# Half-width value products of two attentions, chained into one stretch per group

## The chip, the cores and the metric

The program runs on one NeuronCore of one Trainium2 chip. The engines are named as in the profile: PE is TensorE (matmuls), PEld its weight loads, DVE is VectorE, ACT is ScalarE, POOL is GpSimd, and SP issues most of the DMAs. The metric is the device time of one execution in microseconds (us), lower is better. The kernel before has a median of 2237.99 us over 3 runs (2236.0 to 2239.27).

## What is computed

A sequence of 2048 tokens with 1024 features passes two blocks, all in float32. The first is a gated linear attention (GLA) layer. The second projects the normalised tokens into three mixers, joins their outputs and projects them back. The change lies in two of these mixers, and in a scratch tile of the final projection:

```python
# sliding-window attention: 6 heads in 2 key/value groups of 3, a window of 128
scores = jnp.einsum('bnqkgd,bnskd->bnkgqs', qb, kk) * (A_DH ** -0.5)   # 128 queries x 256 keys
probs = softmax(scores + alibi, with a sink)
out = jnp.einsum('bnkgqs,bnskd->bnqkgd', probs, vv)                    # 64 features a head

# stick-breaking attention: 4 heads of 64, every query against all keys before it
z = jnp.einsum('bhqd,bhsd->bhqs', qb, kh) * (S_DH ** -0.5)
log_keep = jnp.where(strict, jax.nn.log_sigmoid(-z), 0.0)
suffix = lax.cumsum(log_keep, reverse=True) - log_keep
a = jnp.where(strict, jnp.exp(jax.nn.log_sigmoid(z) + suffix), 0.0)
out = jnp.einsum('bhqs,bhsd->bhqd', a, vh)                             # the value product
```

## The kernel before

The tokens go through in 8 tiles of 256. After the GLA block the second block runs as four stages, one behind the other: the sliding-window stage (some 960 to 1250 us of the profiled execution), the mLSTM stage (to some 1635 us), the stick-breaking stage (to 2131 us) and the output projection, half of whose tiles already run beside the last stick-breaking tiles.

Within a stage, `pipeline` sets three streams side by side for each tile: `mix` (the attention of tile t), `gate` (of tile t) and `dense` (the projections of tile t + 1, from `dense3_steps`; in the last tile the first projections of the next stage). The streams are only written interleaved. The order in which each engine gets its instructions is chosen afterwards by a scheduler, which follows the dependences, priorities (`high_priority`) and its own estimate of times. So the dense matmuls on tiles named `mm` fill PE between the attention's steps, and an added ordering edge can move instructions of every engine in that stage. Each engine then works strictly through its list. The dense matmuls use a one-pass 32-bit format (F32R); transposes and value products are plain F32, and each of those stands in the trace as two MATMUL instructions, so x2 in a row is one product or one transpose.

A stick-breaking group (`stick_rows`) is 128 queries, two heads (h = 0 and 1) and up to four key blocks of 128. For each head it makes scores into PSUM (tile `z`, two matmuls of the function `qk`), two sigmoids on ACT (`ke`, `be`), a running product along the keys on DVE (`TENSOR_TENSOR_SCAN` on `ke`), a multiplication into `be` (DVE, every fourth on POOL), up to four PE transposes into the PSUM tile `aT`, and a copy to the SBUF tile `aT`: by ACT for h = 0, by DVE for h = 1, which is made last. Then come the value products, two for each key block. A product takes 128 keys to 64 features, so it uses half the columns of the PE array: head 0 writes partitions 0 to 63 of the PSUM tile `po`, head 1 writes 64 to 127. There are 80 groups: 56 of eight products, and 8 each of six, four and two; 544 products in all. Two streams of groups (b = 0 and 1) are interleaved.

A sliding-window block (`swa_rows`) is 128 queries. Its products are likewise half-width, 128 keys to 64 features, but for three heads at once (384 columns). There are two key blocks (sb) and two key/value groups (kv), so four products a block, and two in the first block; 62 in all. Each takes a transposed tile `pT`, which comes out of PSUM by ACT for kv = 0 and by DVE for kv = 1.

`Bank.mm` issues a product. For the first product on a half of the bank it sets the flag that clears it, and puts every later one of that half behind that first in the order (`behind`: order on the engine alone, no wait). Nothing else orders the products: in the stick-breaking code they are written key block by key block, h = 0 first, and the scheduler may put each wherever its own operand is ready. The sliding-window code issues its products with plain matmuls:

```python
for sb in range(2 - nb, 2):
    for kv in range(2):
        mm(po[kv * 64:kv * 64 + 64, :, :], v[n - 1 + sb][:, kv * 64:kv * 64 + 64], pTs[sb, kv],
           start=sb == 2 - nb, stop=sb == 1)
```

In the output projection (`out2_tiles`) ACT squares the PSUM tile `py` into a scratch tile `ysq`, only for its row sums, and DVE writes `y` from the same PSUM tile.

Of the kernel before, what the change touches and what calls it, by code (L numbers as in the profile page):

```python
# [26 lines left out]
def interleave(a, na, b, nb):  # L27
    """run the generators a (na steps) and b (nb steps) side by side"""
    ia = ib = 0
    while a is not None or b is not None:  # L30
        if b is None or (a is not None and ia * nb <= ib * na):
            if next(a, StopIteration) is StopIteration:
                a = None
            ia += 1
        else:
            if next(b, StopIteration) is StopIteration:
                b = None
            ib += 1


class Bank:
    """accumulation groups side by side in one PSUM bank: its first matmul clears the bank"""
# [4 lines left out]
    def mm(self, out, a, b, stop=False, part=0):  # L47
        first = self.first.get(part)
        i = self.k.nc.tensor.matmul(out, a, b, start=first is None, stop=stop, skip_group_check=True).ins  # L49
        if first is None:  # L50
            self.first[part] = i
        else:
            self.k.behind(i, first)


class ConstPool:
    """single tiles by name"""
# [8 lines left out]
class K:  # L66
# [45 lines left out]
    def open(self, ctx, name, bufs=2, side=None):  # L112
        """SBUF of a phase"""
        return ctx.enter_context(self.tc.tile_pool(name=name, bufs=bufs, side=side, reuse_waits="tile"))

    def psum(self, ctx, name, **banks):
        """the PSUM banks of a phase by tag; mm: beside the two lasting ones"""
# [3 lines left out]
    def behind(self, ins, before):  # L121
        """issue order on one engine, no wait"""
# [3 lines left out]
    def table(self, name):  # L126
        """the activation tables that the following Exp, Ln or Sigmoid use"""
# [22 lines left out]
    def weights(self, src, name, stage=None, pool=None, k0=0, k1=None, more=None):  # L150
        """src: DRAM [128, k, n]; returns the hi and lo parts of rows k0 to k1. stage: gives the staging tiles;
        more: DRAM [128, k, m] of further columns"""
# [24 lines left out]
    def pipeline(self, n, load, dense, nd, gate, ng, mix, nm, first, lead=0, nxt=None, pri=0):  # L177
        """beside mix(t) run gate(t, h of t) and dense(t + 1, h of t + 1); load(t) gives h two tiles ahead.
        nd, ng, nm(t): the steps of dense, gate and mix; lead: gate goes first for so many t;
        first: h of tile 0 and its dense, begun or None. nxt: what follows: its load(0), its weights, its dense  # L180
        and the steps of it that go here; returns h, weights and the dense begun"""
# [36 lines left out]
    def ahead(self, steps, n):  # L218
        """the steps, their instructions picked as if they stood n earlier"""
# [7 lines left out]
    def load_hl(self, src):  # L227
        """src: DRAM hi and lo [128, NK, T] each"""
# [9 lines left out]
    def load_h(self, src, pool, n, bufs, tag="hf"):  # L238
        """src: DRAM [128, NK, T] -> hi, lo; by n rows"""
# [5 lines left out]
    def split_h(self, parts, B=None):  # L245
        """parts: (k, float32 [128, n, T]) -> hi, lo of them, plus the columns B if given"""
# [17 lines left out]
    def dense3(self, out, a, ca, b, cb):  # L264
        """out = sum over k of a[:, k, ca].T @ b[:, k, cb], float32 from three passes."""
# [3 lines left out]
    def dense3_steps(self, out, a, ca, b, cb):  # L269
        """the same, with a stop in the middle"""  # L270
# [9 lines left out]
    def rstd(self, out, ss, n):  # L280
        """out = (ss / n + EPS) ** -0.5"""
# [4 lines left out]
    def silu_col(self, src, n, name):  # L286
        """silu of a [128, n] tile by exp and ln."""
# [8 lines left out]
    def matvec(self, pool, w, c, col0):  # L296
        """acc[p, j] = sum over k of c[k * 128 + p] * w[k * 128 + p, col0 + j], j < 512"""
# [11 lines left out]
    def mod_cols(self, pool, stage, w, c, name, at):  # L309
        """columns: G = g * (1 + scale), B = shift, each [128, NK] (feature k * 128 + p). at: (k, what to do there)"""  # L310
# [43 lines left out]
    def transposed(self, xs, tag):  # L354
        """xs: two [128, D] token tiles -> (k, two rows of 128 features in a PSUM bank)"""
# [8 lines left out]
    def make_h(self, pool, banks, G, B, tags=(("hn", 2),) * 4):  # L364
        """banks: of transposed tokens (already scaled by rstd) -> float32 times the columns G, plus B if given,
        by two rows of 128 features"""
# [15 lines left out]
    def x_rstd(self, wk, i, keep):  # L382
        """token-major x, or its squares, and the rstd of its rows"""
# [20 lines left out]
    def x_normed(self, wk, t, G):  # L404
        """feature-major x times rstd and the columns G, by two rows of 128 features"""
# [12 lines left out]
    def gla_consts(self, wk):  # L418
# [7 lines left out]
        # the gate's low-rank part, token-major: hi, hi, lo, each with a column for the bias  # L426
# [76 lines left out]
    def late_mod(self, wk, j):  # L503
        """512 columns of: gate of block 1, shift, scale and gate of block 2"""
# [28 lines left out]
    def gla_dense(self, wk, t, hs, W, st):  # L533
# [6 lines left out]
        # token-major v and r; the low-rank gate  # L540
# [6 lines left out]
        if t % NT == 0:  # L547
            # its rows from partition 0 and 64: hi, from 32: lo, to meet the gate's hi, lo and hi
# [78 lines left out]
        # v of the second head  # L627
# [8 lines left out]
    def gla_gate(self, wk, t, hs, W, st):  # L636
        """silu of r"""
# [11 lines left out]
    def gla_mix(self, wk, t, st, ST):  # L649
# [4 lines left out]
        # scores of both heads and both 128-token chunks  # L654
# [75 lines left out]
    def units(self, key):  # L730
        """loads of the four weight units of a phase"""
# [3 lines left out]
    def halves(self, W):  # L735
        """units of half the rows -> all rows"""
# [66 lines left out]
    def fm(self, out, W, c0, hs):  # L803
        """feature-major block: out [128 columns from c0, T]"""
        self.dense3(out, W, slice(c0, c0 + 128), hs, slice(0, T))

    def stack_k(self, ka, kb, pk, cols):
        """pk [128, T]: two heads on the partition halves; their hi and lo parts, each head stacked on 128"""
# [6 lines left out]
    def stack_q(self, qs, pq):  # L815
        """pq [128, T]: two heads on the partition halves. qs [128, 4, T]: by head, hi on both halves;
        then by head, lo on the half of its k's hi, zero on the other"""
# [8 lines left out]
    def qk(self, out, qs, h, qt, ks):  # L826
        """out = q.T @ k of head h; ks: columns of its stacked k"""
# [81 lines left out]
    def stick_rows(self, wk, n, b, q, i, kst, v, zero, y, st, po, bank):  # L909
        """queries n * 128 .. of heads 2b and 2b + 1 against all keys before them, from the last chunk back"""  # L910
# [5 lines left out]
        while end > 0:  # L916
# [3 lines left out]
            aTs = []  # L920
            for h in range(2):
# [26 lines left out]
                aT = wk.tile([128, 4, 128], F32, name="aT", tag="aT", bufs=3)  # L948
                if h == 0:
                    nc.scalar.activation(aT[:, 0:nb, :], pa[:, 0:nb, :], AF.Copy)  # L950
                else:
                    nc.vector.tensor_copy(aT[:, 0:nb, :], pa[:, 0:nb, :])  # L952
                aTs.append(aT)
            for j in range(nb):
                for h in range(2):
                    c = (2 * b + h) * 64
                    bank.mm(po[h * 64:h * 64 + 64, :], v[:, s0 // 128 + j, c:c + 64], aTs[h][:, j, :],
                            s0 == 0 and j == nb - 1, h)
# [7 lines left out]
    def silu_exp(self, out, src, tmp):  # L966
        """out = src * sigmoid(src), tmp of the same shape"""
# [99 lines left out]
    def swa_rows(self, wk, n, i, qs, kst, v, bias, sink, y, st):  # L1067
# [48 lines left out]
        for sb in range(2 - nb, 2):  # L1116
            for kv in range(2):
                mm(po[kv * 64:kv * 64 + 64, :, :], v[n - 1 + sb][:, kv * 64:kv * 64 + 64], pTs[sb, kv],
                   start=sb == 2 - nb, stop=sb == 1)
# [4 lines left out]
    def mlstm_stats(self, wk, t, g, mp):  # L1124
        """g: gate pre-activations [128, chunk, 8] of tile t -> per-token exponents by chunk and head:
        for the columns, for the state, exp(-m)"""
# [70 lines left out]
    def mlstm_dense(self, t, hs, W):  # L1197
# [8 lines left out]
        def values():  # L1206
            """v, token-major with a column of ones, and the gates"""
# [50 lines left out]
        # q and k of each head  # L1258
# [50 lines left out]
    def mlstm_chunk(self, wk, c, i, st, Cs, hg):  # L1309
# [44 lines left out]
        # h = num / max(|den|, exp(-m)), normed over the head  # L1354
# [30 lines left out]
    def out2_tiles(self, wk, W, hs, t0, t1, bufs, rstd):  # L1385
# [4 lines left out]
        for t in range(t0, t1):  # L1390
            hn = load(t + 1) if t + 1 < NT else None
            for i in range(2):
# [3 lines left out]
                for half in range(2):  # L1396
# [4 lines left out]
                    sq = wk.tile([128, 512], F32, name="ysq", tag="ysq", bufs=1)  # L1401
# [123 lines left out]
```

## Time and profile before

| | before |
|---|---|
| median of 3 runs | 2237.99 us (2236.0 to 2239.27) |
| profiled execution, span from first to last instruction | 2235.3 us |
| PE busy | 2131.8 us, 95% |
| PE weight loads busy | 1902.3 us, 85% |
| DVE busy | 1356.7 us, 61% |
| ACT busy | 902.1 us, 40% |
| POOL busy | 857.7 us, 38% |

The profile is of one execution. Busy PE time is modelled, since matmuls are pipelined: a row's own duration overlaps the next row's, and what a piece of PE work costs is read from the starts of successive rows. In a timeline, the first number is the start of the first instruction of a row, xN the number of merged instructions, and a bracket at the end is idle time of the engine and what ended it. L49 is the matmul line of `Bank.mm`, L276 to L278 are the three dense matmuls, L829 and L830 the scores, L947 the stick-breaking transposes, L1108 and L1118 the transposes and products of the sliding window.

### The profile page before, as it was taken

How to read it: one execution, taken by the hardware profiler on the slowest of the kernel's cores; microseconds unless marked ns; L12 is line 12 of the kernel's file. 1: busy time of each engine (PE TensorE's matmuls, PEld its weight loads, DVE VectorE, ACT ScalarE, POOL GpSimd, SP SyncE). 2: the span in 40 equal slices, each digit the busy share in tenths (PEclk: the TensorE clock that was granted, in tenths of full speed). 3: DMA queues.
4: the chain of work that ended last, by engine and by line, in shares of the span. 5: the costliest groups of instructions: out<-in, count | busy, mean ns of one | idle time of the engine just before them, and what ended most of it. 6: DMA issues, size and time to landing. Idle time of an engine off the chain costs nothing. (4 is left out here: it accounts for less than half of the span.)

```text
span 2235.3 us, 39197 instructions
## 1 busy us (share of the span) xinstructions
PE 2131.8 (95%) x14912; PEld 1902.3 (85%) x14912; DVE 1356.7 (61%) x2517; ACT 902.1 (40%) x2290; POOL 857.7 (38%) x1362
## 2 busy tenths in 40 slices
PE   6999999999999999899999999889799999999998
PEld 6899998899998788797888898888798888777787
DVE  6755756566656466564545455445456688788843
ACT  3534334333333333354545343433445555554411
POOL 3522335322223455553324322232445454573410
PEclk9999999999999999999999999989899999999999
DMA  9522313423322566751214322332441111122252
GB/s 321 178 67 73 126 55 114 123 82 99 91 67 91 195 210 225 241 165 53 90 46 145 98 65 72 84 99 67 121 130 43 44 44 43 44 67 81 67 175 99
DMA packets 122412, 240.00 MB, mean 107 GB/s; under 512 B 13248, under 2 KB 39782, under 8 KB 122224
## 3 DMA queue, kind: packets, MB, share of 16 engines
q1 hardware_dynamic: 108400, 187.17, 27.1%
q0 software_dynamic: 13824, 50.34, 7.1%
q8 instruction: 117, 1.92, 0.4%
q14 instruction: 71, 0.58, 0.1%
HBM read 178.66 MB, written 58.79 MB: 106 GB/s over the span
## 5 line engine op out<-in xcount | busy, mean ns | idle before, releaser
L937 DVE TENSOR_TENSOR_SCAN ke<-ke,zero 128x512 f32<-128x512 f32 (+3 forms) x160 | 186.9, 1182 | 25.9 <-POOL ke L932 14.1
L276 PE MATMUL mm<-hh,u1h 128*128 128x256 f32 x640 | 189.1, 296 | 0.0
L278 PE MATMUL mm<-hh,u1l 128*128 128x256 f32 x640 | 187.9, 294 | 0.0
L277 PE MATMUL mm<-hl,u1h 128*128 128x256 f32 x640 | 186.6, 292 | 0.0
L276 PE MATMUL mm<-u0h,hh 128*128 128x272 f32 (+2 forms) x464 | 155.1, 334 | 5.7 <-POOL hh L260 3.6
L278 PE MATMUL mm<-u0h,hl 128*128 128x272 f32 (+2 forms) x464 | 153.9, 332 | 0.6 <-DVE hl L261 0.4
L277 PE MATMUL mm<-u0l,hh 128*128 128x272 f32 (+2 forms) x464 | 153.6, 331 | 0.0
L276 PE MATMUL mm<-hh,u2h 128*128 128x256 f32 x512 | 147.3, 288 | 0.8 <-DVE gs L564 0.5
L277 PE MATMUL mm<-hl,u2h 128*128 128x256 f32 x512 | 146.4, 286 | 0.0
L278 PE MATMUL mm<-hh,u2l 128*128 128x256 f32 x512 | 145.7, 286 | 0.0
L278 PEld LDWEIGHTS mm<-hh,u1l 128*128 128x128 f32 x640 | 126.0, 197 | 1.3 <-issue 0.9
L276 PEld LDWEIGHTS mm<-hh,u1h 128*128 128x128 f32 x640 | 126.0, 197 | 0.7 <-issue 0.2
L277 PEld LDWEIGHTS mm<-hl,u1h 128*128 128x128 f32 x640 | 125.6, 196 | 0.7 <-issue 0.3
L276 PE MATMUL mm<-u3h,hh 128*128 128x256 f32 (+1 forms) x384 | 124.3, 324 | 0.8 <-DVE vl L546 0.8
L278 PE MATMUL mm<-u3h,hl 128*128 128x256 f32 (+1 forms) x384 | 123.3, 321 | 0.0
L277 PE MATMUL mm<-u3l,hh 128*128 128x256 f32 (+1 forms) x384 | 122.7, 319 | 0.0
L49 PE MATMUL po<-aT,sv 128*64 128x128 f32 x1088 | 108.9, 285 | 6.6 <-DVE aT L952 4.9
L134 ACT ACTIVATE be<-z 128x512 f32<-128x512 f32 (+3 forms) x160 | 86.0, 538 | 68.3 <-PE aT L947 68.0
L276 PE MATMUL mm<-hh,u3h 128*128 128x256 f32 x384 | 110.4, 287 | 0.5 <-POOL u3h L147 0.5
L277 PE MATMUL mm<-hl,u3h 128*128 128x256 f32 x384 | 110.3, 287 | 0.0
L278 PE MATMUL mm<-hh,u3l 128*128 128x256 f32 x384 | 109.3, 285 | 0.2 <-DVE mprev L1189 0.2
L134 ACT ACTIVATE ke<-z 128x512 f32<-128x512 f32 (+3 forms) x160 | 86.1, 541 | 54.8 <-PE z L830 33.1
(419 smaller groups left out, 6983.9 us busy)
## 6 DMA issues: line engine op xcount, KB each, us to landing
hh<-h2Th POOLq DMA_DIRECT2D x48, 512.0 KB, 6.0
hl<-h2Tl POOLq DMA_DIRECT2D x48, 512.0 KB, 5.3
mvw<-in_mod_w SPq DMA_DIRECT2D x48, 256.0 KB
stage<-in_ada_w SPq DMA_DIRECT2D x32, 256.0 KB
xt<-in_x SPq DMA_DIRECT2D x16, 512.0 KB
stage<-in_gla_w SPq DMA_DIRECT2D x32, 256.0 KB
oT<-oT SPq DMA_DIRECT2D x32, 256.0 KB
hf<-hT SPq DMA_DIRECT2D x32, 256.0 KB
```

What stands on the lines that cost most here:

```text
L49: i = self.k.nc.tensor.matmul(out, a, b, start=first is None, stop=stop, skip_group_check=True).ins
L134: i = self.nc.scalar.activation(out, src, func, **kw).ins
L276: mm(out, ah[k][:, ca], bh[k][:, cb], start=(k == 0), stop=False)
L277: mm(out, ah[k][:, ca], bl[k][:, cb], start=False, stop=False)
L278: mm(out, al[k][:, ca], bh[k][:, cb], start=False, stop=(k == NK - 1))
L937: nc.vector.tensor_tensor_scan(ke[:, 0:w][:, ::-1], ke[:, 0:w][:, ::-1], zero.to_broadcast([128, w]), ke[:, w:w + 1], op0=OP.mult, op1=OP.add)
```

## The change

The value products of a group become one chain. `Bank.mm` returns its instruction and takes another, `after`, behind which the new one is put in PE's order, without a wait. Both attentions hand the last product on to the next. The order within a chain starts at the operand that is made last: in stick-breaking h = 1 before h = 0 for each key block, in the sliding window sb = 1 before sb = 0 and kv = 1 before kv = 0. The half on the array alternates from product to product. The sliding window's products now go through `Bank.mm` too, so their line in a trace becomes L49.

The two SBUF tiles `aT` of a group become one tile with a half for each head, allocated at the start of the group; two such tiles stand in place of three single ones. In the output projection the scratch tile `ysq` goes, and ACT's unused squares are written into `y`, which DVE overwrites afterwards. All docstrings and comments are removed, which moves line numbers by three or more.

```diff
-    def mm(self, out, a, b, stop=False, part=0):
+    def mm(self, out, a, b, stop=False, part=0, after=None):
         first = self.first.get(part)
         i = self.k.nc.tensor.matmul(out, a, b, start=first is None, stop=stop, skip_group_check=True).ins
         if first is None:
             self.first[part] = i
         else:
             self.k.behind(i, first)
+        if after is not None:
+            self.k.behind(i, after)
+        return i
...
-            aTs = []
+            aT = wk.tile([128, 2, 4, 128], F32, name="aT", tag="aT", bufs=2)
...
-                aT = wk.tile([128, 4, 128], F32, name="aT", tag="aT", bufs=3)
                 if h == 0:
-                    nc.scalar.activation(aT[:, 0:nb, :], pa[:, 0:nb, :], AF.Copy)
+                    nc.scalar.activation(aT[:, h, 0:nb, :], pa[:, 0:nb, :], AF.Copy)
                 else:
-                    nc.vector.tensor_copy(aT[:, 0:nb, :], pa[:, 0:nb, :])
-                aTs.append(aT)
+                    nc.vector.tensor_copy(aT[:, h, 0:nb, :], pa[:, 0:nb, :])
+            ins = None
             for j in range(nb):
-                for h in range(2):
+                for h in (1, 0):
                     c = (2 * b + h) * 64
-                    bank.mm(po[h * 64:h * 64 + 64, :], v[:, s0 // 128 + j, c:c + 64], aTs[h][:, j, :],
-                            s0 == 0 and j == nb - 1, h)
+                    ins = bank.mm(po[h * 64:h * 64 + 64, :], v[:, s0 // 128 + j, c:c + 64], aT[:, h, j, :],
+                                  s0 == 0 and j == nb - 1, h, ins)
...
-        for sb in range(2 - nb, 2):
-            for kv in range(2):
-                mm(po[kv * 64:kv * 64 + 64, :, :], v[n - 1 + sb][:, kv * 64:kv * 64 + 64], pTs[sb, kv],
-                   start=sb == 2 - nb, stop=sb == 1)
+        bank, ins = Bank(self), None
+        for sb in range(1, 1 - nb, -1):
+            for kv in (1, 0):
+                ins = bank.mm(po[kv * 64:kv * 64 + 64, :, :], v[n - 1 + sb][:, kv * 64:kv * 64 + 64], pTs[sb, kv],
+                              sb == 2 - nb, kv, ins)
...
-                    sq = wk.tile([128, 512], F32, name="ysq", tag="ysq", bufs=1)
...
-                    nc.scalar.activation(sq, py, AF.Square, accum_out=sm[:, half:half + 1])
+                    nc.scalar.activation(y, py, AF.Square, accum_out=sm[:, half:half + 1])
```

What this does to PE's list, first early in the sliding-window stage. Here `po` takes the products, `pT` the transposes, `sc` the scores and `mm` the dense work; xN counts equal instructions in a row, one for each product. Before:

```order
L276 MATMUL mm<-hh,u2h 128x256
L277 MATMUL mm<-hl,u2h 128x256
L278 MATMUL mm<-hh,u2l 128x256
L1108 MATMUL pT<-ident,s 128x128 x3
L1118 MATMUL po<-pT,av 64x384
L276 MATMUL mm<-hh,u2h 128x256
L277 MATMUL mm<-hl,u2h 128x256
L278 MATMUL mm<-hh,u2l 128x256
L276 MATMUL mm<-hh,u2h 128x256
L1108 MATMUL pT<-ident,s 128x128
L1118 MATMUL po<-pT,av 64x384
L1108 MATMUL pT<-ident,s 128x128 x2
```

After:

```order
L1111 MATMUL pT<-ident,s 128x128
L280 MATMUL mm<-hl,u1h 128x256
L281 MATMUL mm<-hh,u1l 128x256
L279 MATMUL mm<-hh,u1h 128x256
L280 MATMUL mm<-hl,u1h 128x256
L281 MATMUL mm<-hh,u1l 128x256
L49 MATMUL po<-pT,av 64x384 x4
L1111 MATMUL pT<-ident,s 128x128 x3
L279 MATMUL mm<-hh,u1h 128x256
```

The four products of a block stood singly among dense work and transposes, and now stand in a row. Over the whole list the 62 products stood in 61 stretches (60 single products and one pair); now they stand in 16, fifteen of four and one of two.

In the stick-breaking stage, on PE, in the tiles where groups have eight products (`aT` are the transposes where it is written to, and the operand where `po` is written). Before:

```order
L278 MATMUL mm<-u2h,hl 128x256
L276 MATMUL mm<-u2h,hh 128x256
L277 MATMUL mm<-u2l,hh 128x256
L49 MATMUL po<-aT,sv 64x128 x7
L947 MATMUL aT<-ident,be 128x128 x2
L278 MATMUL mm<-u2h,hl 128x256
L276 MATMUL mm<-u2h,hh 128x256
L277 MATMUL mm<-u2l,hh 128x256
L49 MATMUL po<-aT,sv 64x128
L947 MATMUL aT<-ident,be 128x128 x2
```

After:

```order
L281 MATMUL mm<-hh,u0l 128x256
L279 MATMUL mm<-hh,u0h 128x256
L49 MATMUL po<-aT,sv 64x128 x8
L280 MATMUL mm<-hl,u0h 128x256
L281 MATMUL mm<-hh,u0l 128x256
L279 MATMUL mm<-hh,u0h 128x256
L280 MATMUL mm<-hl,u0h 128x256
L950 MATMUL aT<-ident,be 128x128 x4
```

A group's first product (h = 0, first key block) stood alone ahead of the other seven; now the eight stand in one row, at the place that the second head's copy allows. Over the whole list the 544 products stood in 152 stretches, 78 of them a single product and 53 of seven; now in 80, one for each group, 56 of them of eight. In both stages the scheduler has also picked the other instructions anew around these places, on all engines. Ahead of the sliding-window stage, and through the middle of the mLSTM stage, the order of every engine is as it was.

## Rows read from the trace of the kernel before

**Rows 1.** The page: busy us of each engine, share, instructions.

```profile
PE 2131.8 (95%) x14912; PEld 1902.3 (85%) x14912; DVE 1356.7 (61%) x2517; ACT 902.1 (40%) x2290; POOL 857.7 (38%) x1362
```

**Rows 2.** Busy us by stretch: bounds, length, PE, PEld, DVE, ACT, POOL, clock, DMA.

```profile
960.00:1250.00 290.00, 289.23 (x2052) 243.95 (x2051) 154.48 (x349) 138.26 (x412) 109.39 (x182) 1.00 0.30 96
1640.00:1800.00 160.00, 160.00 (x1282) 141.99 (x1281) 103.34 (x162) 77.34 (x179) 77.48 (x178) 1.00 0.18 58
1800.00:2000.00 200.00, 191.09 (x1524) 160.27 (x1523) 169.61 (x217) 110.18 (x237) 114.25 (x221) 0.99 0.17 50
1960.00:2000.00 40.00, 35.39 (x265) 28.93 (x264) 36.88 (x43) 21.30 (x44) 33.20 (x45) 1.00 0.27 80
2000.00:2120.00 120.00, 119.33 (x724) 91.99 (x722) 104.90 (x214) 52.76 (x108) 48.79 (x93) 1.00 0.24 73
```

**Rows 3.** Timeline of PE, stick-breaking: two transposes (x4) among dense matmuls.

```profile
1690.33 0.28 PE L277 MATMUL mm<-u2l,hh 128*128 128x256 f32 x1
1690.45 0.60 PE L947 MATMUL aT<-ident,be 128*128 128x128 f32 x4
1690.81 0.36 PE L278 MATMUL mm<-u2h,hl 128*128 128x256 f32 x1
```

**Rows 4.** The same view: a single product between dense matmuls.

```profile
1698.84 0.28 PE L277 MATMUL mm<-hl,u3h 128*128 128x256 f32 x1
1699.05 0.43 PE L49 MATMUL po<-aT,sv 128*64 128x128 f32 x2
1699.41 0.39 PE L278 MATMUL mm<-hh,u3l 128*128 128x256 f32 x1
1699.63 0.28 PE L276 MATMUL mm<-hh,u3h 128*128 128x256 f32 x1
```

**Rows 5.** The same view: a single product ahead of two transposes.

```profile
1693.34 0.43 PE L49 MATMUL po<-aT,sv 128*64 128x128 f32 x2
1693.70 0.66 PE L947 MATMUL aT<-ident,be 128*128 128x128 f32 x4
1694.11 0.48 PE L829 MATMUL z<-kst,q 128*128 128x512 f32 x1
```

**Rows 6.** The same view: a stretch of seven products, and one of eight.

```profile
1700.43 1.09 PE L49 MATMUL po<-aT,sv 128*64 128x128 f32 x14
1701.45 0.66 PE L947 MATMUL aT<-ident,be 128*128 128x128 f32 x4
...
1957.19 1.09 PE L49 MATMUL po<-aT,sv 128*64 128x128 f32 x16
1958.21 0.33 PE L947 MATMUL aT<-ident,be 128*128 128x128 f32 x1
```

**Rows 7.** Timeline of PE, sliding window: the only pair, then a single product.

```profile
1022.74 0.87 PE L1118 MATMUL po<-pT,av 128*64 128x384 f32 x4
1023.53 0.39 PE L830 MATMUL sc<-akst,q 128*128 128x256 f32 x1
...
1242.81 0.28 PE L278 MATMUL mm<-hh,u2l 128*128 128x256 f32 x1
1243.02 0.86 PE L1118 MATMUL po<-pT,av 128*64 128x384 f32 x2
1243.81 0.39 PE L276 MATMUL mm<-hh,u2h 128*128 128x256 f32 x1
1244.04 0.28 PE L277 MATMUL mm<-hl,u2h 128*128 128x256 f32 x1
```

**Rows 8.** Line L49: instructions, min/median/max ns, first and last start.

```profile
L49 PE MATMUL po<-aT,sv x1088: 272/273/476, 1645.2 to 2130.6; 128*64 128x128 f32 x182
```

**Rows 9.** Timeline of SP: loads of the mLSTM stage's weights.

```profile
1211.58 31.23 SPq L165 DMA_DIRECT2D stage<-in_e_w  x10
```

**Rows 10.** Timeline of DVE in the output projection.

```profile
2213.72 0.69 DVE L1407 TENSOR_TENSOR y<-mm,gg 128x512 f32<-128x512 f32 x1 [3.21 <-ACT ysq L1404]
```

**Rows 11.** Whom PE waited for, 1645 to 2131 us: total us, times, longest.

```profile
PE po L49 <- DVE aT L952: 4.9, 5, 1.6
```

## Prediction

> **What bounds the kernel now.** I read the page first: PE is busy for 95% of the span, the next engine, DVE, for 61% [rows 1]. That is an average, so the busy time of stretches came next. In the sliding-window stage PE is busy 289 of 290 us and DVE 154. In the first third of stick-breaking it is 160 of 160 against 103; from 1800 us on DVE climbs to 170 of 200 and PE begins to wait, with 35.4 busy of 40 and DVE at 36.9 in its worst stretch [rows 2]. So PE sets the pace of both stages that the change touches, and late in stick-breaking DVE is close behind. The timeline of PE then has to tell what the products cost it, by the starts of successive rows.
>
> **A product that stands alone.** An instruction starts 0.12 us behind a dense matmul of 256 columns [rows 3]. Round a single stick-breaking product the starts run 1698.84, 1699.05, 1699.41, 1699.63 [rows 4]: 0.79 us from the dense matmul ahead to the second one behind it, where two steps of 0.12 would be 0.24. The product takes 0.55 us out of PE's time: 0.09 late at its start, 0.36 to the next instruction, 0.10 late behind it. Ahead of transposes it is a little less: the transposes take 0.36 us without it and 0.41 behind it, so 0.09 + 0.36 + 0.05 = 0.50 [rows 3, 5].
>
> **A product in a stretch.** Seven products in a row take 1.02 us to the next instruction and eight take 1.02 as well [rows 6]: one on the other half of the array runs beside its neighbour. From one product (0.36) to seven, which is three pairs more, it is 0.66 us, or 0.22 for each further pair. In the sliding window the one pair that stands together takes 0.79 us, 1022.74 to 1023.53, and a single product also takes 0.79, 1243.02 to 1243.81 [rows 7]. There, too, the second is free.
>
> **Stick-breaking, what goes from PE.** By the order, 78 products stand alone before, and none after; there are 80 stretches where 152 were. Of the 72 stretches that vanish nearly all are singles that join their own group's seven (or five, or three) at no price. In the timeline, whose products run from 1645.2 to 2130.6 us [rows 8], 44 of the 78 singles stand ahead of transposes and 34 do not: 44 x 0.50 + 34 x 0.55 = 40.7 us, of which 72 in 78 go: 38 us. By stretches of time (28 of the singles before 1800, 33 from 1800 to 2000, 17 behind) that is 14, 16 and 8 us.
>
> **How much of it the span gives back.** Before 1800 us all 14: DVE would be busy 103 us of 146. From 1800 to 2000, DVE's 170 us would have to fit in 184, a share of 92%. The highest share in rows 2 is also 92%, but PE waited there; with 87%, from 2000 to 2120, it hardly did [rows 2]. At a limit of 87% the stretch falls to 195 us and gives 5; at 92% it gives all 16. I take 10, the middle, as DVE's wait chain and not its sum decides there. Behind 2000 us the bounds are 0 and 8 by the same two shares, and I take 4. Stick-breaking gives 28 us, between 19 and 38.
>
> **Sliding window, what goes from PE.** A single product between dense matmuls costs 1.23 - 0.24 = 0.99 us (1242.81 to 1244.04) [rows 7], and I count the 39 of the 60 that stand ahead of transposes 0.05 lower, as in stick-breaking. Sixty singles and the pair come to 58 us. A stretch of four costs the pair's 0.96 and one further pair. No row shows that one. Its bounds are three times the 0.22 above, since it has 384 columns for 128, which is 0.66, and a whole pair of 0.79. I take 0.70, nearer the stretches that rows show. Fifteen such stretches and the first block's pair come to 15 x 1.66 + 0.96 = 26 us. So 32 us go (31 to 33). No other engine is near its limit: DVE would have 154 us of 258 [rows 2]. The last tile is different. Beside its two blocks (4 us of the 32) the weights of the mLSTM stage come in, ten loads in 31 us, one behind the other [rows 9], and dense work on them is what fills PE; I count half of those 4. The stage gives 30 us. What follows it, the mLSTM stage, has the same order as before and should only start earlier.
>
> By the Trainium skill (TensorEngine Tiling (Array Packing), Theoretical Speedup) operands of at most 64 columns give up to 2x. By that rule alone, with nothing for the switch in and out of half-width work, a block's four products would go from 4 x 0.79 to 2 x 0.79 us; that is 24 us in place of 32. The rows have the switches as well, about 0.2 us each time, so I stay with them.
>
> **The other edits.** The new order edges are no waits. The joint `aT` tile holds two groups where three single tiles held one and a half, so a copy waits for older products than before: nothing added. In the output projection the write of `y` now has to wait for ACT's square; the trace shows that it does so already, DVE's L1407 is released by ACT's `ysq` [rows 10]: nothing. Line numbers cost nothing.
>
> **The sum.** 28 + 30 = 58 us off the span of 2235.3 gives 2177. The median of the runs lies 2.7 us above that span, so the forecast is **2180 us**.
>
> **Rivals.**
>
> *PE's whole saving comes through.* 38 + 32 = 70 us: 2168. For it: PE was full wherever the singles stood, and the few waits on the second head's copy could shrink as well. Against it: DVE at 92% late in stick-breaking.
>
> *DVE holds stick-breaking.* At the limit of 87% the stage gives 19 us and the sum is 49: 2189. For it: PE already loses 4.6 us of 40 where DVE stands at 92%.
>
> *The sliding window's buffers hold it.* All four `pT` tiles of a block now stay taken until its stretch, where each single product used to free one. The next block's copies then wait, and its transposes behind them on PE. At 1 us a block, the size of the waits on an operand in the other stage [rows 11], this takes 15 of the 30 us: 2195. For it: the order puts the next block's first transposes ahead of the stretch. Against it: there is dense work enough between, and ACT and DVE are half idle.
>
> *A whole stretch waits for the last operand, slower than before.* In the old order a single product on the first head's operand could go early; now nothing of a group runs until the second head's copy is there, and in PE's list everything behind it stands still. The trace has this wait now, 4.9 us in five times, about 1 us each [rows 11]. If each of the 96 stretches (80 and 16) met it, 96 us would be lost against 70 gained: 2264. It decides from 70 / 96 = 0.73 us a stretch. Against it: the seven already waited for the same copy, and only 5 in 80 groups showed a wait. The Trainium skill (TensorE: Matmul & The Clock Gate, Part 3: Packing small matmuls) has the rule behind this one: matmuls start and end in strict order, and only weight loads are pulled ahead. The trace agrees so far as PE does stand idle ahead of such products [rows 11].
>
> *It doesn't do what it says.* If the halves did not run beside each other once chained, nothing would change: 2238. The pair and the stretch of eight speak against it.
>
> **How the numbers follow.** Chances: the forecast 0.44, the whole saving 0.19, DVE holding stick-breaking 0.19, the sliding window's buffers 0.10, no effect 0.03, slower 0.05. The forecast's own bounds, by the limits above, are some 2172 to 2186. The range must reach the whole saving at 2168 with some us below it, for waits that go too, and the two rivals at 2189 and 2195 with some us above: 2162 to 2202. Outside lie no effect, slower, and two rivals together. About 0.2% (4.5 us) is what a measurement of this kernel can tell from no change. Faster by more than that has 0.44 + 0.19 + 0.19 + 0.10 = 0.92, the same 0.03, slower 0.05.
>
> **What would show it right or wrong.** In the changed kernel's timeline the sliding window's stretches should be x8 rows that take 1.45 to 1.6 us to the next instruction, and stick-breaking's x16 rows 1.02. The sliding-window stage should end some 30 us earlier, and the mLSTM stage last as long as it did. The last stick-breaking product should come near 2073 us, where it came near 2131 [rows 8]. DVE's share should rise to about 90% late in stick-breaking, with PE's waits there on `aT`, `be` or `ke` some 10 us longer than now. I would be wrong if the x8 rows take over 2 us (no pairing), if PE waits at the head of most stretches, or if the mLSTM stage takes back what the sliding window gave.

## The result

The changed kernel takes 2199.01 us (median of four runs, 2194.68 to 2201.77) where the kernel before takes 2237.09 beside it: a ratio of 0.9823, 95% interval 0.9807 to 0.9838. It is 38 us faster. The forecast was 2180, 58 us faster, with a range of 2162 to 2202. The profiled execution of e11, the last but one of the runs below, was in a slow state, so that run has a ratio and no stage lengths.

The page of the changed kernel, busy time of each engine, against [rows 1]:

```profile
span 2193.0 us, 39218 instructions
PE 2066.5 (94%) x14912; PEld 1882.8 (86%) x14912; DVE 1352.9 (62%) x2517; ACT 898.3 (41%) x2290; POOL 861.5 (39%) x1362
```

PE has 65 us less busy time, but the span is only 42 us shorter. Where the stages begin and end is read from first and last starts (the two numbers behind the comma): of the sliding window's products, of stick-breaking's score matmuls and of its products. First the kernel before:

```profile
L1118 PE MATMUL po<-pT,av x124: 486/512/538, 996.7 to 1250.1; 128*64 128x384 f32 x124
L829 PE MATMUL z<-kst,q x160: 221/394/541, 1635.2 to 2108.1; 128*128 128x512 f32 x112, 128*128 128x128 f32 x16, 128*128 128x256 f32 x16, 128*128 128x384 f32 x16
```

Then the changed kernel (the last row answers to [rows 8]):

```profile
L49 PE MATMUL po<-pT,av x124: 486/486/537, 999.5 to 1226.4; 128*64 128x384 f32 x124
L832 PE MATMUL z<-kst,q x160: 221/392/775, 1612.1 to 2067.8; 128*128 128x512 f32 x112, 128*128 128x128 f32 x16, 128*128 128x256 f32 x16, 128*128 128x384 f32 x16
L49 PE MATMUL po<-aT,sv x1088: 272/273/473, 1622.7 to 2093.8; 128*64 128x128 f32 x182
```

| us of the profiled executions | before | after | difference |
|---|---|---|---|
| start to the first sliding-window product | 996.7 | 999.5 | +2.8 |
| sliding-window products, first to last | 253.4 | 226.9 | -26.5 |
| from there to the first stick-breaking score | 385.1 | 385.7 | +0.6 |
| stick-breaking and projection, from that score to the end | 600.1 | 580.9 | -19.2 |

The first row is code that the change leaves in its order; over the other runs below it lies between 998 and 1004 us. The mLSTM stage neither gives nor takes. So the sliding window gave 26.5 us for a forecast of 30, and stick-breaking with the projection 19 for 28.

What PE pays for a stretch is as forecast. All 15 sliding-window stretches of four and nearly all 56 stick-breaking stretches of eight are alike to 0.01 us. The timeline of PE in the changed kernel, sliding window and stick-breaking, against [rows 4 to 7]:

```profile
1056.08 0.28 PE L279 MATMUL mm<-hh,u2h 128*128 128x256 f32 x1
1056.28 1.51 PE L49 MATMUL po<-pT,av 128*64 128x384 f32 x8
1057.72 0.39 PE L832 MATMUL sc<-akst,q 128*128 128x256 f32 x1
...
1721.07 0.28 PE L279 MATMUL mm<-hh,u0h 128*128 128x256 f32 x1
1721.28 1.09 PE L49 MATMUL po<-aT,sv 128*64 128x128 f32 x16
1722.30 0.39 PE L280 MATMUL mm<-hl,u0h 128*128 128x256 f32 x1
1722.53 0.28 PE L281 MATMUL mm<-hh,u0l 128*128 128x256 f32 x1
```

Four sliding-window products take 1.44 us to the next instruction (1056.28 to 1057.72) and eight stick-breaking ones 1.02. The further pair in the sliding window costs 1.44 - 0.79 = 0.65, at the lower of its two bounds.

In the sliding window PE's busy time and its waits tell where the 26.5 us come from. Stretches as in [rows 2], first of the kernel before, then two of the changed one:

```profile
996.70:1250.10 253.40, 253.40 (x1758) 208.84 (x1757) 130.76 (x292) 119.69 (x355) 86.88 (x131) 1.00 0.27 85
999.50:1226.40 226.90, 222.76 (x1757) 204.93 (x1758) 138.05 (x291) 118.89 (x353) 87.75 (x131) 0.99 0.29 95
1200.00:1226.40 26.40, 22.35 (x162) 19.81 (x162) 17.48 (x30) 9.14 (x25) 14.63 (x18) 0.94 0.39 131
```

PE was never idle there before; now it is idle for 4.1 us, all but 0.1 of it in the last tile, behind 1200 us. There the granted clock is 0.94 as well, which costs 0.06 x 26.4 = 1.6 us.

In stick-breaking the rest is in the waits. Whom PE waited for, 1595 to 2095 us (total us, times, longest):

```profile
PE po L49 <- DVE aT L954: 9.6, 8, 2.5
PE mm L279 <- DVE y L1410: 3.8, 2, 3.2
PE z L832 <- ACT be L137: 2.7, 2, 2.5
PE aT L950 <- DVE be L944: 2.6, 5, 0.8
PE tr L1374 <- POOL hn L1369: 1.0, 1, 1.0
PE mm L279 <- DVE sm L1423: 1.0, 2, 0.6
```

These come to 20.7 us. The list of the kernel before held [rows 11] and three more:

```profile
PE z L829 <- ACT be L134: 2.3, 1, 2.3
PE po L49 <- DVE ys L963: 1.6, 2, 1.4
PE mm L276 <- DVE y L1407: 0.7, 1, 0.7
```

With its 4.9 that is 9.5, so 11 us are new. Most of the idle time lies between 1840 and 2000 us. Busy time of PE, PEld, DVE, ACT and POOL in stretches of the changed kernel, then granted clock and DMA, against [rows 2]:

```profile
1760.00:1840.00 80.00, 80.00 (x712) 72.44 (x711) 67.45 (x98) 49.17 (x111) 43.81 (x103) 1.00 0.20 61
1840.00:2000.00 160.00, 144.30 (x1085) 120.78 (x1084) 137.81 (x203) 76.60 (x164) 96.46 (x168) 0.96 0.19 54
2000.00:2093.00 93.00, 89.67 (x576) 71.99 (x574) 77.14 (x169) 37.23 (x80) 29.32 (x58) 0.98 0.25 77
```

The clock's column has a part that the prediction left out. In the changed kernel PE stands idle for 2.5 us and then finds its clock at the lower level for some 10 us. After the second wait shown it does so for some 3 us, and once more after a third, of 2.3 us, at 2084 us:

```profile
1940.63 0.49 PE L832 MATMUL z<-kst,q 128*128 128x512 f32 x1 [2.46 <-ACT be L137]
1985.57 0.80 PE L279 MATMUL mm<-u0h,hh 128*128 128x512 f32 x1 [3.18 <-DVE y L1410]
...
1936.00:1940.00 4.00, 2.17 (x10) 1.47 (x8) 3.97 (x3) 0.54 (x1) 4.00 (x4) 1.00 0.61 166
1940.00:1944.00 4.00, 2.82 (x19) 2.04 (x20) 3.04 (x5) 3.22 (x8) 3.57 (x5) 0.65 0.31 87
1944.00:1948.00 4.00, 3.36 (x12) 2.55 (x13) 3.55 (x5) 2.07 (x4) 3.66 (x4) 0.50 0.04 12
1948.00:1952.00 4.00, 4.00 (x12) 3.16 (x11) 3.49 (x6) 0.21 (x1) 1.75 (x5) 0.57 0.20 54
1984.00:1988.00 4.00, 2.43 (x6) 1.95 (x7) 4.00 (x9) 2.66 (x5) 2.96 (x6) 0.70 0.20 75
1988.00:1992.00 4.00, 4.00 (x21) 3.04 (x21) 4.00 (x6) 0.00 (x0) 1.60 (x3) 0.88 0.26 66
```

The column before the last two is the granted clock: 1.00 is 2.4 GHz and 0.50 is 1.2 GHz. From 1840 to 2093 us the means of 0.96 and 0.98 say that some 13 + 4 = 17 us ran at the lower level, which takes half of that, 8 us. In the kernel before, the stretches from 1640 to 2120 us lost some 2 us so [rows 2]. The sum closes: of the 38 us that the forecast took from PE, 11 came back as waits and some 7 through the clock, and 20 are left for the 19 measured. PE's busy time in the last stage bears it out (before, then after):

```profile
1635.20:2235.30 600.10, 584.51 (x4066) 488.50 (x4064) 428.56 (x704) 259.90 (x588) 252.82 (x518) 1.00 0.24 75
1612.10:2193.00 580.90, 555.11 (x4066) 479.06 (x4064) 421.07 (x704) 255.48 (x588) 255.67 (x518) 0.98 0.25 77
```

It fell by 29.4 us although the lower clock stretched it by 7, so some 36 us of work went; its idle time rose from 15.6 to 25.8.

### The profile page after: what moved, and what is told of

It reads as the page before. It is cut to its first block, busy times and chain, and to the rows that moved or that the text cites. A ratio compares the mean times of both kernels' runs of the same rounds, so it can differ in the third digit from the quotient of the medians.

```text
span 2193.0 us, 39218 instructions
## 1 busy us (share of the span) xinstructions
PE 2066.5 (94%) x14912; PEld 1882.8 (86%) x14912; DVE 1352.9 (62%) x2517; ACT 898.3 (41%) x2290; POOL 861.5 (39%) x1362
## 5 line engine op out<-in xcount | busy, mean ns | idle before, releaser
L940 DVE TENSOR_TENSOR_SCAN ke<-ke,zero 128x512 f32<-128x512 f32 (+3 forms) x160 | 180.7, 1143 | 19.6 <-POOL ke L935 11.5
L279 PEld LDWEIGHTS mm<-u0h,hh 128*128 128x128 f32 x464 | 88.6, 191 | 20.5 <-POOL hh L263 4.6
```

Of the source, the lines that this page charges most:

```text
L279: mm(out, ah[k][:, ca], bh[k][:, cb], start=(k == 0), stop=False)
L940: nc.vector.tensor_tensor_scan(ke[:, 0:w][:, ::-1], ke[:, 0:w][:, ::-1], zero.to_broadcast([128, w]), ke[:, w:w + 1], op0=OP.mult, op1=OP.add)
```

## The experiments

All stand beside runs of the kernel before on the same chip; a ratio is to those. The stage lengths are of one profiled execution each, from the rows named above.

| us | window | to score | score to end | ratio, 95% interval |
|---|---|---|---|---|
| before | 253.4 | 385.1 | 600.1 | 1 |
| after | 226.9 | 385.7 | 580.9 | 0.9823 (0.9807, 0.9838) |
| e1 sliding window alone | 225.8 | 385.5 | 600.0 | 0.9879 (0.9863, 0.9896) |
| e2 stick-breaking alone | 253.2 | 387.2 | 579.5 | 0.9892 (0.9877, 0.9908) |
| e3 scratch tile back | 227.3 | 389.5 | 582.1 | 0.9799 (0.9775, 0.9823) |
| e4 both copies on ACT | 226.1 | 385.7 | 572.0 | 0.9767 (0.9752, 0.9782) |
| e5 same half in a row | 225.6 | 387.3 | 602.1 | one run, 2215.74 us |
| e6 old order of operands | 253.3 | 384.1 | 597.4 | 0.9979 (0.9967, 0.9991) |
| e7 before, more DVE work | 253.3 | 383.2 | 608.7 | 1.0037 (1.0019, 1.0054) |
| e8 after, more DVE work | 225.9 | 386.2 | 596.9 | 0.9869 (0.9848, 0.9890) |
| e9 e4, last scaling on DVE | 227.8 | 385.4 | 572.6 | 0.9765 (0.9748, 0.9783) |
| e10 four be buffers | 226.4 | 388.7 | 576.3 | 0.9776 (0.9756, 0.9796) |
| e11 all three | | | | 0.9758 (0.9740, 0.9775) |
| e12 two by two | 225.9 | 385.4 | 581.7 | 0.9797 (0.9776, 0.9818) |

The runs of after and those of e1 to e12 were taken on different occasions. e3 and e12 have its stage lengths, but measure 0.980 where it measures 0.982; the intervals overlap. e1 to e12 are best compared among themselves. A stage length comes from one execution, which need not be a typical one: e3's, at 2203.09 us, lies well above its median, and e4's, at 2184.86, below.

**e1, the sliding window alone.** The stick-breaking code and the projection are as before.

> The sliding-window chain alone: stick-breaking and the projection's scratch tile as before. Theory (PE time freed in a stage that PE bounds is kept): the trace of the changed kernel has the sliding window's last product 24 us earlier, so some 2212 us (2207 to 2217). Rival (the mLSTM stage or the later stages take it back through weights that arrive no earlier): above 2225.

Measured 2213.9 us, inside the band. The window is 27.6 us shorter, and everything behind it lasts as before, to 0.4 us. The rival falls.

**e2, stick-breaking alone.** The sliding-window code and the scratch tile are as before.

> The stick-breaking chain alone: sliding window and scratch tile as before. Theory (38 us leave PE, about 13 come back as waits late in the stage and 7 through a lower granted clock behind such waits): 18 to 20 us saved, 2218 us (2212 to 2224). Rival (the loss comes from the new sliding-window order or from the scratch tile, not from the chain): 30 us or more saved, below 2207.

Measured 2217.02 us; the last stage is 20.6 us shorter. By the stage lengths the two parts add up, 27.6 + 20.6 against 26.5 + 19.2 in the changed kernel, so stick-breaking's loss is its own. By the medians e1 and e2 save 26.3 and 23.2 us, which is more than e3, with both, saves beside the same runs (44.8); the intervals are too wide to tell the two sums apart. The waits of e2 are the changed kernel's, for the same tiles:

```profile
PE po L49 <- DVE aT L954: 8.1, 6, 2.5
PE mm L279 <- DVE y L1410: 4.0, 3, 3.1
PE aT L950 <- DVE be L944: 2.7, 5, 0.8
PE z L832 <- ACT be L137: 2.7, 1, 2.7
```

**e3, the scratch tile back.** The changed kernel with

```diff
+                    sq = wk.tile([128, 512], F32, name="ysq", tag="ysq", bufs=1)
...
-                    nc.scalar.activation(y, py, AF.Square, accum_out=sm[:, half:half + 1])
+                    nc.scalar.activation(sq, py, AF.Square, accum_out=sm[:, half:half + 1])
```

> The changed kernel with the scratch tile ysq restored, so that ACT's squares no longer wait until the output DMA has left the tile y (13 us in four waits in the changed kernel's trace). If that wait is on the path: 5 to 8 us faster than the changed kernel, 2192 us. If it is not, as the prediction has it: within 3 us of the changed kernel, 2196 to 2202.

The changed kernel shows a wait that the prediction had not seen. Whom ACT waited for, 1900 to 2095 us:

```profile
ACT y L1407 <- DMA out<-y: 13.4, 4, 6.5
```

In e3 that wait is gone, and the last stage lasts 582.1 us for 580.9; in e2, which also has the scratch tile, it lasts 579.5. The median of 2195.45 lies between the two expectations, with single runs from 2190 to 2203, and 0.9799 (0.9775 to 0.9823) cannot be told from the changed kernel's 0.9823. So the wait is real, and no step was found that it holds; a cost of some 3 us is not excluded.

**e4, both copies on ACT.** As e3, with

```diff
-                if h == 0:
-                    nc.scalar.activation(aT[:, h, 0:nb, :], pa[:, 0:nb, :], AF.Copy)
-                else:
-                    nc.vector.tensor_copy(aT[:, h, 0:nb, :], pa[:, 0:nb, :])
+                nc.scalar.activation(aT[:, h, 0:nb, :], pa[:, 0:nb, :], AF.Copy)
```

> As e3, and the second head's copy out of PSUM runs on ACT like the first head's, which takes 80 copies, some 48 us, from DVE and gives about as much to ACT. Theory (DVE's share of 87% sets the pace late in stick-breaking): 10 to 18 us faster than e3, near 2183. Rival (waits come from chains through ACT and the arrival of weights, or from the order, not from DVE's load): no gain over e3 or slower, 2195 to 2208.

Measured 2189.84 us, 5.6 below e3, and a last stage 10 us shorter than e3's in the profiled executions. The two intervals overlap a little, but e9, which has the same stick-breaking code, repeats both: 2187.84 us and a last stage of 572.6. The gain is less than expected and more than none. The stretch of the lost clock:

```profile
1840.00:2000.00 160.00, 147.29 (x1178) 124.66 (x1176) 132.71 (x182) 98.69 (x214) 104.51 (x179) 0.99 0.18 52
```

DVE has 5 us less to do there and PE 3 us more done, and the clock is at 0.99 for 0.96, worth 0.03 x 160 = 5 us. The waits did not go. They moved to the step ahead of the copy, the multiplication into `be`, which is mostly DVE's too (whom PE waited for):

```profile
PE aT L950 <- DVE be L944: 10.3, 11, 2.3
PE po L49 <- ACT aT L951: 2.2, 2, 1.8
PE aT L950 <- POOL be L944: 1.3, 1, 1.3
```

**e5, products of one half in a row.**

```diff
-            for j in range(nb):
-                for h in (1, 0):
+            for h in (1, 0):
+                for j in range(nb):
...
-        for sb in range(1, 1 - nb, -1):
-            for kv in (1, 0):
+        for kv in (1, 0):
+            for sb in range(1, 1 - nb, -1):
```

> The changed kernel with the same chains, but all products of one half first, then all of the other, so that neighbours no longer alternate. Theory (most of a stretch's cheapness comes from neighbours on different halves running beside each other): a product then costs some 0.32 us, an x16 row takes 2.6 us where it took 1.02, a sliding-window x8 row 3.0 where it took 1.44; some 105 + 24 us more, 2330 us. Rival (the gain is that the switch into half-width work is paid once a stretch, whatever follows whatever): rows as in the changed kernel, 2199 us.

Both theories missed. It took 2215.74 us, not 2330 and not 2199. Timeline of PE, a sliding-window row and a stick-breaking one:

```profile
1046.90 1.52 PE L49 MATMUL po<-pT,av 128*64 128x384 f32 x8
1048.35 0.55 PE L1111 MATMUL pT<-ident,s 128*128 128x128 f32 x3
...
1673.63 1.58 PE L49 MATMUL po<-aT,sv 128*64 128x128 f32 x16
1675.14 0.66 PE L950 MATMUL aT<-ident,be 128*128 128x128 f32 x4
```

Four products, two of each half in a row, cost 1.45 us, nothing over the changed kernel. Eight, four of each half in a row, cost 1.51 where they cost 1.02. The starts of the instructions in such rows of e5, in ns from the first, tell why:

```
four products, two and two (8 instructions):     0, 14, 374, 387, 696, 710, 1019, 1032
eight products, four and four (16 instructions): 0, 160, 269, 378, 487, 493, 597, 654, 706, 763, 815, 872, 982, 1091, 1200, 1309
```

In the first row the starts come in pairs, and the pairs over 300 ns apart. The second instruction starts 14 ns behind the first, though the next three in the list are of the first one's half. In the second row instructions of one half are never less than 109 ns apart. So the one at 14 ns must be of the other half, from further down the list; the trace doesn't name the half, so this is a reading of the starts. In the second row five instructions start alone, and the second stream begins at 493 ns, when three of the first half's eight are still to start. So PE does not start matmuls strictly in order: one on an idle half goes ahead of up to three that wait for the busy half. e12 tests this.

The run serves a second end. PE has 56 x 0.49 + 8 x 0.27 = 30 us more work in stick-breaking than in the changed kernel (0.27 is the loss of the groups of six), and the last stage is 21 us longer. A microsecond on PE is worth 0.7 us there.

**e6, the chain with the old order of operands.**

```diff
-                for h in (1, 0):
+                for h in range(2):
...
-        for sb in range(1, 1 - nb, -1):
-            for kv in (1, 0):
+        for sb in range(2 - nb, 2):
+            for kv in range(2):
...
```

> The changed kernel with the chain but the old order of operands (h = 0 first; sb = 0 and kv = 0 first). In PE's list 77 stick-breaking products and 60 sliding-window ones stand alone again. Theory (what counts is that the chain begins at the last operand, since a chain alone only orders): the time of the kernel before, 2230 to 2240 us. Rival (the chain itself, or the joint tile, already gives part): 2200 to 2225.

Measured 2235.19 us, 0.2% below the kernel before, with its stage lengths to within 3 us. The chain alone orders and doesn't gather: the first operand is ready early, the scheduler puts its product where it is ready, and the rest stands elsewhere. The gain comes from beginning at the operand made last.

**e7 and e8, more DVE work.** The kernel before and the changed kernel, each with

```diff
                     nc.vector.tensor_copy(...)
+                    nc.vector.tensor_tensor(self.dum[:, 0:w], self.dum[:, 0:w], self.dum[:, 0:w], op=OP.mult)
```

> The kernel before with one DVE multiplication more in each stick-breaking group, on a scratch tile that nothing reads: 80 of up to 0.68 us, some 46 us, of which 38 in the last four tiles. Theory (PE sets the pace, DVE has some room): 5 to 20 us slower, 2245 to 2260. If DVE has no part in it: no change.

> The changed kernel with the same additional DVE work. Theory (from about 1840 us on DVE sets the pace of stick-breaking): the 38 us of the last four tiles are nearly all paid, 25 to 40 us slower, 2224 to 2239, and clearly more than the kernel before pays for them. Rival (waits come from chains and the order, DVE's load is not the limit): as much as the kernel before, 5 to 20 us, 2204 to 2219.

The kernel before lost 8.6 us in its last stage (2246.85 us, 0.37% in all), inside e7's band of 5 to 20. The changed kernel lost 16.0 (2210.52 us), which is the rival's band in e8, though it pays about twice as much: 0.35 us for each of the 46 added, where the kernel before paid 0.19. DVE's load matters more than before and is not the limit, or the 38 us in the last four tiles would have come back nearly whole.

**e9, the last tile's scaling on DVE.** As e4, with

```diff
-            nc.gpsimd.tensor_tensor(ss[g][:, :, lo:], ss[g][:, :, lo:],
+            (nc.vector if n >= 14 else nc.gpsimd).tensor_tensor(ss[g][:, :, lo:], ss[g][:, :, lo:],
```

> As e4 (scratch tile restored, both copies on ACT), and in the last sliding-window tile the probabilities are scaled by DVE and not by POOL. In the changed kernel's trace PE waits 3.2 us for that scaling, which stands in POOL's list behind a split that itself waits 4.4 us for a weight load of the next stage. Theory (that list is what takes back the last tile's saving): 3 to 5 us faster than e4, near 2186. Rival (the weights themselves hold the last tile): as e4, within 2 us.

In the changed kernel POOL and PE showed, in the last sliding-window tile:

```profile
1202.81 0.62 POOL L150 TENSOR_SCALAR u2h<-stage 128x512 fp32r<-128x512 f32 x1 [4.41 <-DMA stage<-in_e_w]
1203.40 3.48 POOL L1102 TENSOR_TENSOR s<-s,den 128x512 f32<-128x512 f32 x3
1204.49 0.69 PE L1111 MATMUL pT<-ident,s 128*128 128x128 f32 x2 [3.16 <-POOL s L1102]
```

With the scaling on DVE this wait shrinks to 0.5 us, and PE waits a little later instead:

```profile
1210.29 0.55 PE L1108 MATMUL pT<-ident,s 128*128 128x128 f32 x3 [1.85 <-DVE pT L1113]
1212.84 0.90 PE L1108 MATMUL pT<-ident,s 128*128 128x128 f32 x3 [1.73 <-ACT pT L1111]
```

Measured 2187.84 us and a ratio of 0.9765 for e4's 0.9767: no gain. The rival holds as to the time. That the weights' arrival is what holds this tile fits, but was not tried by itself.

**e10, four buffers for `be`.**

```diff
-name="be", tag="be", bufs=3
+name="be", tag="be", bufs=4
```

> The changed kernel with four buffers for the tile be where it has three. In its trace ACT waits 45 us late in stick-breaking for transposes on PE to free a be. Theory (the late waits come from too few groups in flight, a chain through be, and not from DVE's load): 6 to 15 us faster than the changed kernel, 2184 to 2193. Rival (no buffer limits it): 2195 to 2202.

Measured 2190.88 us; the last stage is 4.6 us shorter than the changed kernel's. Beside e12, which has the changed kernel's stage lengths and stood in the same runs with 2194.77 us, it gains 3.9. That lies in the theory's band, but it is not clear of the noise: the ratios are 0.9776 (0.9756 to 0.9796) and 0.9797 (0.9776 to 0.9818). ACT's wait for a free `be` fell from 44.9 to 28.1 us, but PE gained little by it: it waits 14.6 us for the second head's copy, in ten places, where the changed kernel waits 9.6 in eight. So a gain by the buffer is not shown.

**e11, all three.** e9's two moves and e10's buffer, without the scratch tile.

> The changed kernel with e9's two moves (both copies on ACT, the last tile's scaling on DVE) and e10's four be buffers, without the scratch tile. If the three act on different waits: 2172 to 2184. If the copies on ACT and the buffers act on the same waits: as e9, 2184 to 2190.

The ratio is 0.9758 (0.9740 to 0.9775), some 2186 us: with e4 and e9 at 0.977 nothing that these runs can tell apart. The buffer adds nothing measurable to the copies on ACT. That fits two changes that act on the same waits, and as well a buffer that does nothing. It is the lowest ratio of the study, and like e4 and e9 0.3 to 0.4% below e3.

**e12, two by two.** Two products of one half, then two of the other.

```diff
-            for j in range(nb):
-                for h in (1, 0):
+            for j0 in range(0, nb, 2):
+                for h, j in ((h, j) for h in (1, 0) for j in range(j0, min(j0 + 2, nb))):
```

> The changed kernel with the stick-breaking chain in the order of two products of one half, then two of the other. From e5, where the second half's products began while three instructions of the first half still had to start: if PE starts a matmul on the idle half ahead of up to three that wait on the busy half, an x16 row takes 1.02 to 1.05 us to the next instruction, as in the changed kernel, and the time is 2199 us. If matmuls start strictly in order, only one pass in four overlaps, the row takes 1.4 to 1.7 us and the time is some 15 us longer, 2214 us.

Timeline of PE:

```profile
1854.35 1.14 PE L49 MATMUL po<-aT,sv 128*64 128x128 f32 x16
1855.42 0.77 PE L950 MATMUL aT<-ident,be 128*128 128x128 f32 x5
```

1.07 us, a hair above the band and far from the 1.4 of a strict order. The time of 2194.77 us is the changed kernel's. Of the two expectations in e12, the order with look-ahead is the one that came.

## Why the prediction came out as it did

**What PE pays for the products was right.** A free second product, 0.22 for each further pair and 1.66 for a sliding-window stretch of four: the rows of the changed kernel agree to a few hundredths. The price of a single cannot be read there, since none is left, but PE's work fell by some 32 us in the sliding window and 36 in the last stage, where the forecast had 32 and 38. e6, with the chain, the joint tile and no scratch tile, gains next to nothing, so the gain comes from where the products stand.

**The sliding window was right, a little high.** 30 forecast, 26.5 measured, 27.6 in e1. The 32 us left PE, and 4 came back as waits in the last tile, where the prediction had given back 2. In the profiled execution the lower clock behind such a wait took 1.6 more; in e1 it did not. The mLSTM stage, as forecast, only began earlier.

**Stick-breaking was the mis-sized term:** 28 forecast, 19 measured, at the lower of its bounds. The prediction took 38 us from PE and gave back 10 of them late in the stage, 6 before 2000 us and 4 behind. About 36 us of work went, and PE's idle time rose by 10.2: both terms came out in size. The step that failed is a term that is not in the sum: PE's clock, put at nothing without a word. Waits of 2.3 to 3.2 us left PE at 1.2 GHz for about 17 us in all, where the kernel before had some 4, and this cost 7 us.

That the 10 us came out is in part luck, and so is the 19 that the limit of 87% on DVE's share gives, since that limit holds no clock. The prediction's own sign, a share of about 90%, did not appear: DVE was busy 86% from 1840 to 2000 us and 83% from there to 2093, where the kernel before had 85% and 87% [rows 2]. (By its share of 92% the upper bound behind 2000 us is 6 us and not 8, too: 104.9 / 0.92 is 114 of 120.) What sets the waits is not settled. e8 shows DVE work paid at a third of its size, and e4 takes DVE out of the copy and finds PE waiting for `be` instead. A group's steps pass PE, ACT, DVE, POOL and PE again. That with PE shorter this chain shows at whichever step is late fits these runs, but no run removed it, and which step would have to go for the rest stays open.

**The other edits were right in time.** Leaving out the scratch tile costs nothing that e3 can tell from noise, although the step was incomplete: ACT's squares into `y` now wait for the output DMA as well. The joint `aT` tile held nothing: among the waits of ACT and DVE in stick-breaking there is none for an older product to free it.

**The rivals.** The whole saving didn't come; PE's waits grew. DVE holding stick-breaking, at 2189, was the nearest in mechanism, with the reservation above. The sliding window's buffers, at 2195, lie nearer by the number alone, but they held next to nothing: PE waited 0.9 us for ACT's copies, not 15. Stretches that wait for the last operand cost 9.6 us in eight places, not 96. So the time lies inside the range, but 20 of the forecast's 58 us did not come, and the last stick-breaking product started at 2093.8 us and not near 2073. Of the 19 us between 2180 and 2199, 9 are stick-breaking, 3.5 the sliding window, 3 the untouched stages ahead in the profiled execution, and the rest that this execution lies 6 us below the median, where before it was 2.7.

## What to carry to other kernels

Read what a short matmul costs from the starts of its neighbours, ahead of it and behind it, not from its own row: here the switch into and out of half-width work cost about 0.3 us, an estimate from a single's 0.55 less the 0.22 of a further pair, and 0.99 less 0.65 in the sliding window. Gathering four sliding-window products took them from some 3.9 us to 1.6. Here an order edge gathered instructions only where it began at the operand that is ready last. And where PE is full but other engines are close behind, don't count on all of the freed time: here half of it came through. Look in such a stretch for the lower clock behind PE's waits: it took 7 us here, behind waits of 2.3 to 3.2 us.

## What the hardware showed that was not expected

The text ahead of the prediction says that each engine works strictly through its list. By these starts PE does not: half-width matmuls do not always start in the order of the list. A matmul on the idle half of the array started 14 ns behind the first of its row while three on the busy half stood ahead of it (e5), and two-by-two order costs 1.07 us for eight products where alternation costs 1.02 and four in a row 1.51 (e5, e12). The Trainium skill (TensorE: Matmul & The Clock Gate, Part 3: Packing small matmuls) states strict order in start and end; the starts measured here differ from it. The prediction's rival from that rule concerned waits for an operand. There the trace goes with it: PE stood idle for 9.6 us ahead of products whose operand was late.
